# A two-layer GDN/mLSTM trunk on one core: the end written out in TensorE's order, the GDN heads' merge moved, and the second norm's factors two steps on

## The chip, the cores and the metric

The kernel runs on one core of a Trainium2 chip. The metric is the device time of one execution in microseconds (us). Its engines are TensorE (PE in the rows; its weight loads are PEld), VectorE (DVE), ScalarE (ACT), GpSimd (POOL) and SyncE (SP, which issues DMAs; SPq is the DMA queue it feeds). Each engine runs its own list of instructions in order and waits where an operand or a buffer is not ready.

## What is computed

Two residual layers over a sequence of 1024 tokens of width 1024, and a last RMSNorm. Layer 0 is a gated DeltaNet (GDN), layer 1 an mLSTM; each has 8 heads with keys of 128 and values of 256.

```python
for i in range(DEPTH):                       # 2
    h = rmsnorm(x, norm_w[i])
    x = x + (gdn_mixer if i % 2 == 0 else mlstm_mixer)(h, ...)
return rmsnorm(x, final_norm_w)
# gdn, chunked: per head and chunk
kk = einsum(k, k); a = I + tril(beta * kk * L, -1)
u, wk = triangular_solve(a, beta * v), triangular_solve(a, beta * exp(gc) * k)
attn = einsum(q, k) * L
w = u - wk @ S;  o = (q * exp(gc)) @ S + attn @ w;  S = decay * S + kd.T @ w     # scan
y = (rmsnorm(o) * silu(z)) @ w_out
```

## The kernel before

Tokens lie along the free axis in two halves of 512 (`half` 0 and 1), the width in eight blocks of 128 rows (`y0_0` to `y7_1` are the residual stream, block and half). A product in full precision is made of three matmuls on split operands (`hi`·`hi`, `lo`·`hi`, `hi`·`lo`) of 512 columns, over the blocks of the contraction.

The projections of all heads are one long row of such matmuls. Three of them are one **step**. After each step a planner, a table of step numbers per head (`KEYS`, `QUERIES`, `SOLVE`, `MERGE`, `TOKENS`, `SCAN`), lets generators issue a piece of the small work of that head: `gdn_keys` (transposes `tpk`, products `kk`, the decay matrix `nt`), `gdn_queries` (transposes `tpq`, their squares `sqrq` on ScalarE, products `kq`), `gdn_solve` (the inverse of the 32x32 diagonal blocks on VectorE, stored with the DMA `tb_dram` and read back as `td`), `gdn_merge` (per half: VectorE makes `tt` and `t` out of `td`, then four small products `xp`, `yp`, `xl`, `yl` put the blocks together, four steps apart), and `gdn_scan` of the head before (`ks`, `y`, `sn`, `o`, and `go`, which transposes the gated output). Each table has three entries: head 0, head 1 and heads 2 to 7. So the order of TensorE's instructions is the program's (`tc.manual_schedule` for PE), and the order on the other engines comes from a scheduler.

A PSUM bank tag names a pool of banks: `"d"` has two banks, `"c"` two and `"b"` one. `tpk`, `kk`, `tpq`, `kq`, `xp` to `yl`, `go` and the output products `out` all take turns on the two banks of `"d"`: a product waits until its bank's last reader is done.

`NORM1` holds the steps at which the second norm's column sums, factors and rows are issued, per half, in layer 0's output products; `prenorm` then needs its row product `n_rs`.

The end: the last head's output product of each block (`out_part`, `out`) and the other seven heads' (`out_heads`, `lout`, whose weights are split by ScalarE into `lw_hi` and by POOL into `lw_lo`) are added to the residual stream on VectorE. `finish(c0, c1)` is the last RMSNorm of columns c0 to c1 (of 8 blocks of 128 tokens): squares on ScalarE, their sum over the eight blocks on POOL (c0 of 0 and 4) or VectorE (6), a column sum on TensorE (`f_cs`), the factor (`f_rc`, with POOL's power), a diagonal matrix (`f_diag`), its row product (`f_rs`), and the multiplies with a DMA of each block. Here TensorE's order is the scheduler's; the program gives the order of the parts, in words whose letter o is `out_part`, h `out_heads` of half 1, a and b the two parts of `finish`:

```python
ORDER = "o0 a0 h1 b0 o4 a4 o6 a6 b4 b6"
```

The functions that the change touches, with the profile's line numbers:

Of the kernel before, what the change touches and what calls it, by code (L numbers as in the profile page):

```python
# [68 lines left out]
def hybrid_kernel(ctx, tc, x_in, norm_w, final_norm_w, gdn_w_in, gdn_conv_w, gdn_a_log, gdn_dt_bias, gdn_norm_w,  # L69
# [1330 lines left out]
    def finish(c0, c1):  # L1400

        ts, n = slice(c0 * P, c1 * P), c1 - c0
        accs = squares_of(c0, n, f"f{c0}", "k", QB, PF[c0])
# [6 lines left out]
        for k in range(KT):  # L1410
            if k in PM[c0]:
                G.tensor_tensor(x_of(k, c0, n), x_of(k, c0, n), rs_sb, ALU.mult)
            else:
                V.tensor_tensor(x_of(k, c0, n), x_of(k, c0, n), rs, ALU.mult)  # L1414
            nc.sync.dma_start(out[k * P:(k + 1) * P, ts], x_of(k, c0, n))
        yield
# [145 lines left out]
    sources.append(out_weights(mlstm_w_out, heads, (wp, "wraw", WB), "lw1"))  # L1562
    starts = [0] + [end for end, _ in LASTENDS]
    parts = {c0: finish(c0, c1) for c0, c1 in zip(starts, starts[1:])}
    for o in ORDER.split():
        if o[0] == "h":
            run(loads[1])
            run(out_heads(1, heads, gss[1], "lout"))
        elif o[0] == "o":
            c0 = int(o[1:])  # L1570
            out_part(st, c0, {0: 4, 4: 2, 6: 2}[c0])
        else:
            next(parts[int(o[1:])])
# [52 lines left out]
```

## Time and profile before

| what | value |
|---|---|
| time, median of 3 runs | 1971.52 us (1967.94 to 1972.74) |
| the profiled execution | 1967.29 us, span 1965.6 us |
| mean granted TensorE clock | 0.993 |
| busy: PE, DVE, ACT, POOL | 96%, 65%, 51%, 35% of the span |

The profile is of one execution, whose time is 0.65 us under the lowest of the three timed runs. Busy time is a sum of instruction durations; the span is from the first to the last instruction. The clock is TensorE's granted one as a share of 2.4 GHz. A row's idle time in brackets is that of its engine right before it.

### The profile page before, as it was taken

What the parts mean: (1) busy time and instruction counts of PE and PEld (TensorE: products, weight loads), DVE (VectorE), ACT (ScalarE), POOL (GpSimd) and SP (SyncE); (2) the same over time, 40 slices, a digit from 0 to 9 for tenths busy, and PEclk for the clock granted to TensorE, in tenths of its full rate; (3) what the DMA queues carried; (4) which work ended last, traced back from release to release, by engine and by line L of the source; (5) the groups of instructions that cost most, each with busy time, mean ns of one, the idle gap of its engine ahead of it and who ended that gap; (6) DMA issues with size and microseconds to landing.
All of it is one profiled execution on the core that took longest, in us unless ns stands there. A gap on an engine that the chain in (4) does not pass through costs nothing.

```text
span 1965.6 us, 28818 instructions
## 1 busy us (share of the span) xinstructions
PE 1886.7 (96%) x9768; PEld 1550.2 (79%) x9768; DVE 1271.1 (65%) x2877; ACT 1006.8 (51%) x2325; POOL 692.7 (35%) x621
## 2 busy tenths in 40 slices
PE   5998999999999999999999999999999999999987
PEld 3786787878787878787888788888888888878876
DVE  6678686858595959547555866666666666673313
ACT  5536454646465555545445554545554645564423
POOL 4234334333333334100121333333433333355553
PEclk9999999999999999999999999999999999999999
DMA  4211122121222222636421221212121221246332
GB/s 141 87 42 49 54 71 78 58 75 57 79 63 67 65 67 77 197 109 232 122 86 56 78 74 59 73 57 82 61 80 63 70 68 65 81 137 205 105 119 76
DMA packets 138620, 171.24 MB, mean 87 GB/s; under 512 B 30860, under 2 KB 68584, under 8 KB 138472
## 3 DMA queue, kind: packets, MB, share of 16 engines
q1 hardware_dynamic: 138472, 169.40, 27.5%
q8 instruction: 77, 1.26, 0.3%
q14 instruction: 71, 0.58, 0.1%
HBM read 142.87 MB, written 26.48 MB: 86 GB/s over the span
## 4 chain that ended last, share of the span: by engine, by line
PE 77%; DVE 10%; DMA 4%; ACT 3%; issue 2%; POOL 1%; SPq 1%; DVEq 0%; ACTq 0%; POOLq 0%
PE lout L679 8%; PE gkv_ps L480 7%; PE gout L679 7%; PE mkq_ps L480 7%; PE mv_ps L480 7%; PE mz_ps L480 6%; PE mog_ps L480 6%; PE gqv_ps L480 5%; PE gzp_ps L480 4%; PE mo L1455 1%; PE mv_ps L1212 1%; PE gv_ps L480 1%; PE o L1040 1%; PE y L1023 1%; PE out L384 1%
## 5 line engine op out<-in xcount | busy, mean ns | idle before, releaser
L394 POOL TENSOR_TENSOR g_r<-g_r,mhalf 128x1 f32<-128x1 f32 x64 | 41.4, 647 | 212.5 <-DVE g_r L393 192.4
L268 DVE SCALAR_TENSOR_TENSOR gw_lo<-gw_raw,rest,gw_hi 128x256 fp32r<-128x256 f32 x128 | 61.3, 516 | 66.0 <-ACT gw_hi L267 66.0
L263 POOL TENSOR_TENSOR lw_lo<-lw_raw,lw_hi 128x512 fp32r<-128x512 f32 x56 | 72.9, 1304 | 73.4 <-ACT lw_hi L262 69.9
L679 PE MATMUL lout<-lgp_hh,lw_hi 128*128 128x512 f32 x224 | 88.7, 396 | 4.6 <-DVE y L1414 3.2
L263 POOL TENSOR_TENSOR mog_lo<-mog_raw,mog_hi 128x512 fp32r<-128x512 f32 x39 | 50.3, 1290 | 115.3 <-ACT mog_hi L262 115.3
L263 POOL TENSOR_TENSOR mz_lo<-mz_raw,mz_hi 128x512 fp32r<-128x512 f32 x39 | 53.8, 1379 | 99.7 <-ACT mz_hi L262 99.7
L267 ACT ACTIVATE gw_hi<-gw_raw,rest 128x256 fp32r<-128x256 f32 x128 | 58.0, 501 | 58.3 <-PE gout L679 42.3
L679 PE MATMUL lout<-lgp_hl,lw_hi 128*128 128x512 f32 x224 | 87.7, 392 | 0.0
L679 PE MATMUL lout<-lgp_hh,lw_lo 128*128 128x512 f32 x224 | 86.8, 392 | 0.0
L263 POOL TENSOR_TENSOR mv_lo<-mv_raw,mv_hi 128x512 fp32r<-128x512 f32 x38 | 51.4, 1353 | 84.1 <-ACT mv_hi L262 53.1
L263 POOL TENSOR_TENSOR gkv_lo<-gkv_raw,gkv_hi 128x512 fp32r<-128x512 f32 x40 | 52.8, 1322 | 78.3 <-ACT gkv_hi L262 67.8
L480 PE MATMUL gkv_ps<-hh,gkv_hi 128*128 128x512 f32 x176 | 78.9, 448 | 0.0
L263 POOL TENSOR_TENSOR gzp_lo<-gzp_raw,gzp_hi 128x512 fp32r<-128x512 f32 x38 | 49.7, 1307 | 66.8 <-ACT gzp_hi L262 55.4
L262 ACT CAST lw_hi<-lw_raw 128x512 fp32r<-128x512 f32 x56 | 34.7, 620 | 73.7 <-PE lout L679 48.9
L263 POOL TENSOR_TENSOR mkq_lo<-mkq_raw,mkq_hi 128x512 fp32r<-128x512 f32 x35 | 45.6, 1302 | 75.9 <-ACT mkq_hi L262 64.8
L480 PE MATMUL gkv_ps<-hh,gkv_lo 128*128 128x512 f32 x176 | 69.2, 393 | 0.0
L480 PE MATMUL gkv_ps<-hl,gkv_hi 128*128 128x512 f32 x176 | 69.0, 392 | 0.0
L679 PE MATMUL gout<-glp_hh,gw_hi 128*128 128x512 f32 x160 | 66.7, 417 | 0.0
L394 POOL TENSOR_TENSOR m_r<-m_r,mhalf 128x1 f32<-128x1 f32 x64 | 42.6, 665 | 66.2 <-DVE m_r L393 65.2
L679 PE MATMUL gout<-glp_hl,gw_hi 128*128 128x512 f32 x160 | 62.7, 392 | 0.0
L679 PE MATMUL gout<-glp_hh,gw_lo 128*128 128x512 f32 x160 | 62.7, 392 | 0.0
L1043 ACT ACTIVATE gv_h<-o,g_r 128x256 f32<-128x256 f32 x64 | 30.3, 473 | 62.5 <-POOL g_r L394 61.8
(769 smaller groups left out, 6688.0 us busy)
## 6 DMA issues: line engine op xcount, KB each, us to landing
gw_raw<-in_gdn_w_out_dram SPq DMA_DIRECT2D x64, 256.0 KB, 2.7
lw_raw<-in_mlstm_w_out_dram SPq DMA_DIRECT2D x56, 256.0 KB, 2.7
gzp_raw<-in_gdn_w_in_dram SPq DMA_DIRECT2D x32, 256.0 KB, 3.2
...
```

What stands on the lines that cost most here:

```text
L262: A.copy(hi, raw)
L263: (e or G).tensor_tensor(lo, raw, hi.bitcast(F32), ALU.subtract)
L267: A.activation(hi[:, k], raw[:, k], AF.Copy, scale=c)
L268: V.scalar_tensor_tensor(lo[:, k], raw[:, k], c, hi.bitcast(F32)[:, k], ALU.mult, ALU.subtract)
L384: mm(ps, a[:, e, ds], b[:, e, hs], start=m == 0, stop=m == 3 * ET - 1)
L394: G.tensor_tensor(r, r, mhalf[:, :1], ALU.pow)
L480: mm(ps, w_[:, k, :], h_, start=first and k == 0 and i == 0, stop=k == 3 and i == 2, skip_group_check=True)
L679: mm(pss[2 * j + i], a[:, e, i * P:(i + 1) * P], b, start=h == heads[0] and e == 0 and m == 0, stop=h == heads[-1] and e == ET - 1 and m == 2)
L1023: mm(yp[:, :DV], st["tt"][half][:, cc, :], rr, start=True, stop=True)
L1040: mm(op[:, :DV], st["at"][half][:, cc, :], w, start=S is None, stop=True)
L1043: A.activation(v, op[:, :DV], AF.Copy, scale=r)
L1212: mm(ps[c], h_[k][half][:, c * P:(c + 1) * P], w_[:, k % 2, :], start=k == 0 and i == 0, stop=k == KT - 1 and i == 2)
```

## The change

Three things are changed.

1. **The end.** TensorE's order is now the program's there too: `out_part` 0 in one piece, then half 1's `lout` with the column sums and the row product of `finish(0, 4)` put between its groups of three matmuls (after 21 and after 51 of them), its multiplies and stores one by one after that; `out_part` 4; `out_part` 6 with the two products of `finish(4, 6)` inside; then `finish(6, 8)`. The sums and rows take banks of tag `"c"` in place of `"b"`. For `finish(6, 8)` the squares of blocks 6 and 7 are not added on VectorE: TensorE sums three parts per column (into `"c"` and `"d"`), and the factor is made per column. Its stores of odd blocks go out on ScalarE's DMA queue.
2. **The GDN tables.** The step numbers of `KEYS`, `QUERIES`, `SOLVE`, `MERGE`, `TOKENS` and `BLOCKS`.
3. **`NORM1`.** The first half's rows are asked for at step 8 in place of 6.

```diff
-NORM1 = ((-1, 4, 6), (-1, 9, 15))
+NORM1 = ((-1, 4, 8), (-1, 9, 15))
-ORDER = "o0 a0 h1 b0 o4 a4 o6 a6 b4 b6"
+F0STEPS = 6, 16
-KEYS = ((4, 9, 11, 14), (28, 31, 32, 35), (22, 25, 26, 29))
-QUERIES = ((17, 20, 22, 30), (68, 71, 76, 76), (82, 82, 86, 91))
-SOLVE = (27, 44, 32)
-MERGE = ((78, 82), (86, 93), (86, 100))
-TOKENS = ((37, 37, 81, 85), (71, 74, 97, 103), (64, 68, 107, 110))
+KEYS = ((2, 7, 8, 15), (32, 35, 36, 39), (22, 25, 26, 29))
+QUERIES = ((17, 20, 23, 30), (68, 71, 76, 76), (80, 80, 84, 89))
+SOLVE = (24, 44, 32)
+MERGE = ((78, 82), (86, 89), (88, 100))
+TOKENS = ((37, 37, 81, 85), (71, 74, 97, 103), (64, 74, 107, 110))
-BLOCKS = (101, 115, 114, 132)
+BLOCKS = (101, 115, 114, 126)
...
+            if k in own:
+                accs[k] = sq
+            elif e in accs:
-                e.tensor_tensor(accs[e], accs[e], sq, ALU.add)
...
+    def column_sums(accs, name, tags):
+        css = [pwork(f"{name}_cs{c}", tag)[:, :1] for c, tag in enumerate(tags)]
+        for i, acc in enumerate(accs):
+            for c, cs in enumerate(css):
+                mm(cs, acc[:, c * P:(c + 1) * P], ones[:, :1], start=i == 0, stop=i == len(accs) - 1)
+        return css
...
-    def finish(c0, c1):
+    def finish(c0, c1, after=None):
+        own = (6, 7) if c1 == NT else ()
...
+        yield
+        sums = column_sums(accs, f"f{c0}", "cd") if own else sums_of(accs, f"f{c0}", "c")
+        diag = rstd_of(sums, f"f{c0}", bool(own))
+        yield
+        rs = rows_of(diag, f"f{c0}", "c")
...
+        with tc.issue_after(after()) if after else nullcontext():
+            for k in range(KT):
...
+                (nc.scalar if own and k % 2 else nc.sync).dma_start(out[k * P:(k + 1) * P, ts], x_of(k, c0, n))
+                if c1 <= HT:
+                    yield
...
+    with tc.manual_schedule(engines={mybir.EngineType.PE}):
+        sources.append(out_weights(mlstm_w_out, heads, (wp, "wraw", WB), "lw1"))
+        run(loads[1])
+        f0, f4, f6 = finish(0, 4), finish(4, 6, lambda: added[0].ins), finish(6, 8)
+        run(out_part(st, 0, 4))
+        do(f0)
+        for n, _ in enumerate(out_heads(1, heads, gss[1], "lout")):
+            if n == F0STEPS[0]:
+                do(f0)
+            if n >= F0STEPS[1] and n % 2 == 0:
+                do(f0)
+        run(out_part(st, 4, 2))
+        do(f4)
+        for n, _ in enumerate(out_part(st, 6, 2)):
+            if n in (1, 5):
+                do(f4)
+        do(f6); do(f6); run(f4); run(f6)
```

In the rows below a tile's name carries head and half or chunk (`xp4_0`: head 4, half 0; `ks3_7`: head 3, chunk 7).

**First place, merge of heads 2 to 7, here head 4.** TensorE before, from the transpose `go3_5` of head 3's scan on (left out are eight and three 512-column matmuls of head 4's projection):

```order
L356 MATMUL go3_5_gp_5296<-ident_117,gv3_h1_4526 128x128 x2
L480 MATMUL gzp4_ps7_5204<-hh0_4_1_425,gzp4_4_hi_5205 128x512
...
L480 MATMUL gzp4_ps7_5204<-hh0_6_1_435,gzp4_4_lo_5206 128x512
L971 MATMUL xp4_0_5314<-t4_0_5250,nt4_0_4624 32x32 x8
L849 MATMUL tpq4_1_5326<-ident_117,gqT4_1_5063 128x128 x4
...
L1018 MATMUL ks3_7_5344<-S3_6_5285,gkT3_1_3444 128x256
```

And now:

```order
L372 MATMUL go3_5_gp_5291<-ident_117,gv3_h1_4526 128x128 x2
L500 MATMUL gzp4_ps7_5204<-hh0_4_1_425,gzp4_4_hi_5205 128x512
...
L869 MATMUL tpq4_1_5308<-ident_117,gqT4_1_5063 128x128 x4
...
L500 MATMUL gzp4_ps7_5204<-hh0_7_1_440,gzp4_4_lo_5206 128x512
L1038 MATMUL ks3_7_5332<-S3_6_5280,gkT3_1_3444 128x256
L500 MATMUL gkv5_ps00_5336<-hh0_0_0_233,gkv5_00_hi_5232 128x512
L500 MATMUL gkv5_ps00_5336<-hl0_0_0_234,gkv5_00_hi_5232 128x512
L500 MATMUL gkv5_ps00_5336<-hh0_0_0_233,gkv5_00_lo_5233 128x512
L991 MATMUL xp4_0_5346<-t4_0_5304,nt4_0_4624 32x32 x8
L500 MATMUL gkv5_ps00_5336<-hh0_1_0_238,gkv5_00_hi_5232 128x512
...
L940 MATMUL kq4_1_5361<-gqT4_1_5063,gkT4_1_4472 128x128 x4
```

`tpq4_1` and `ks3_7` now stand ahead of `xp4_0`, which six more 512-column matmuls precede as well, and `kq4_1` comes three matmuls behind it. On ScalarE at the same place, before (the last products' reads `xs`, the squares `sqrq`, the scan's output `gv3_h1`):

```order
L392 ACTIVATE g3_6_sq_5291,g3_6_r_5290<-o3_6_5287 128x256
L1043 ACTIVATE gv3_h1_4526<-o3_6_5287,g3_6_r_5290 128x256
L977 COPY xs4_0_5323<-xp4_0_5314 32x128
L852 ACTIVATE sqrq4_1_5331,sq4_5254<-tpq4_1_5326 128x128 x2
L262 CAST gkv5_02_hi_5351<-gkv5_raw1_5000 128x512
L852 ACTIVATE sqrq4_1_5331,sq4_5254<-tpq4_1_5326 128x128 x2
```

And now:

```order
L412 ACTIVATE g3_6_sq_5286,g3_6_r_5285<-o3_6_5282 128x256
L872 ACTIVATE sqrq4_1_5313,sq4_5243<-tpq4_1_5308 128x128 x2
L1063 ACTIVATE gv3_h1_4526<-o3_6_5282,g3_6_r_5285 128x256
L872 ACTIVATE sqrq4_1_5313,sq4_5243<-tpq4_1_5308 128x128 x2
L278 CAST gkv5_02_hi_5339<-gkv5_raw1_5000 128x512
L997 COPY xs4_0_5355<-xp4_0_5346 32x128
```

Two of the four squares of `tpq4_1` now run ahead of the scan's scaled copy `gv3_h1`, two behind it, and `xs4_0` comes last.

**Second place, head 1's keys.** VectorE before, up to head 1's first `nt` (`kd1` multiplies `tpk1_0` out of its bank, `hs` are sums of the shared operands, `b1` and `nb1` small factors):

```order
L886 TENSOR_SCALAR nb1_1427<-b1_1425 128x4
L458 TENSOR_TENSOR hs1_1_1760<-hs1_1_1760,x1_0_77 128x512
L299 SCALAR_TENSOR_TENSOR gvT1_0_1_1476<-gkv1_ps11_1279,gcw_159,gvT1_0_1_1476 128x509
L301 TENSOR_TENSOR gvT1_0_1_1476<-gvT1_0_1_1476,gv1_0_edge_285 128x3
L894 SCALAR_TENSOR_TENSOR nt1_0_1493<-kk1_0_1488,nb1_1427,at1_0_1443 128x128 x4
L873 TENSOR_TENSOR kd1_1429<-tpk1_1_1520,ekd_277 128x512
L883 TENSOR_SCALAR sk1_1424<-sk1_1424 128x4
```

And now:

```order
L898 TENSOR_TENSOR at1_1_1549<-growb01_1_1547,cmask_128 128x512
L458 TENSOR_TENSOR S2hl1_1773<-hs1_1_1760,S2hh1_1772 128x512
L893 TENSOR_TENSOR kd1_1476<-tpk1_0_1477,ekd_277 128x512
L903 TENSOR_SCALAR sk1_1471<-sk1_1471 128x4
L477 TENSOR_TENSOR hs2_0_1789<-x2_1_80,x2_0_79 128x512
L904 RECIPROCAL b1_1472<-sk1_1471 128x4
L478 TENSOR_TENSOR hs2_1_1790<-hs2_1_1790,x2_0_79 128x512
L905 TENSOR_TENSOR b1_1472<-b1_1472,beta_273 128x4
L906 TENSOR_SCALAR nb1_1474<-b1_1472 128x4
L914 SCALAR_TENSOR_TENSOR nt1_0_1519<-kk1_0_1514,nb1_1474,at1_0_1490 128x128 x4
```

`kd1` of `tpk1_0` stood sixteen rows ahead of `nt1_0` and now stands seven rows ahead of it, behind three of the shared sums.

**Third place, the end.** TensorE before around the two products of `finish(0, 4)` (`f0_cs`, `f0_rs`):

```order
L384 MATMUL out4_1_19304<-mg7_1_lo_18021,wo0_hi_18141 128x256
L384 MATMUL out4_1_19304<-mg7_1_hi_18020,wo0_lo_18142 128x256
L223 MATMUL f0_cs_18662<-ones_122,f0_sq0_18631 128x1 x4
L242 MATMUL f0_rs_18672<-f0_diag_18670,ones_122 128x512
L679 MATMUL lout1_02_18760<-lgp1_00_hh_18676,lw1_1_0_hi_18770 128x512
L679 MATMUL lout1_02_18760<-lgp1_00_hl_18677,lw1_1_0_hi_18770 128x512
```

And now:

```order
L699 MATMUL lout1_03_18751<-lgp1_00_hh_18571,lw1_1_0_lo_18761 128x512
L235 MATMUL f0_cs_18797<-ones_122,f0_sq0_18717 128x1 x4
L699 MATMUL lout1_03_18751<-lgp1_01_hh_18577,lw1_1_0_hi_18760 128x512
...
L699 MATMUL lout1_00_18748<-lgp1_20_hh_18595,lw1_0_2_lo_18813 128x512
L258 MATMUL f0_rs_18855<-f0_diag_18805,ones_122 128x512
L699 MATMUL lout1_00_18748<-lgp1_21_hh_18601,lw1_0_2_hi_18812 128x512
```

They stood in one place with nothing between them, ahead of half 1's `lout` (apart from what the scheduler had put further ahead); now `lout` matmuls stand ahead of, between and behind them. VectorE before, from the multiplies of columns 4 and 5 to the factor `f6_rc`:

```order
L1414 TENSOR_TENSOR y1_1_18425<-y1_1_18425,f4_rs_19399 128x256
...
L1414 TENSOR_TENSOR y6_1_18435<-y6_1_18435,f4_rs_19399 128x256
L386 TENSOR_TENSOR y7_1_18437<-y7_1_18437,out6_7_19457 128x256
L1414 TENSOR_TENSOR y7_1_18437<-y7_1_18437,f4_rs_19399 128x256
L212 TENSOR_TENSOR f6_sq0_19465<-f6_sq0_19465,f6_sq6_19482 128x256
L212 TENSOR_TENSOR f6_sq0_19465<-f6_sq0_19465,f6_sq7_19485 128x256
L230 TENSOR_SCALAR f6_rc_19499<-f6_cs_19496 128x2
```

And now:

```order
L404 TENSOR_TENSOR y7_1_18437<-y7_1_18437,out6_7_19459 128x256
L1440 TENSOR_TENSOR y1_1_18425<-y1_1_18425,f4_rs_19449 128x256
...
L1440 TENSOR_TENSOR y7_1_18437<-y7_1_18437,f4_rs_19449 128x256
L244 TENSOR_SCALAR f6_rc_19504<-f6_cs0_19496 128x1
L244 TENSOR_SCALAR f6_rc_19504<-f6_cs1_19497 128x1
L251 TENSOR_TENSOR f6_diag_19508<-ident_117,f6_rc_19504 128x256
```

The two additions of squares are gone, `y7_1`'s addition of `out6_7` stands ahead of the multiplies, and the factor is made in two instructions.

## Rows read from the trace of the kernel before

**Rows 1.** Part 1 of the page: each engine's busy time, its share of the span, and its instructions.

```profile
PE 1886.7 (96%) x9768; PEld 1550.2 (79%) x9768; DVE 1271.1 (65%) x2877; ACT 1006.8 (51%) x2325; POOL 692.7 (35%) x621
```

**Rows 2.** The waits of TensorE over the whole span. Columns: the instruction that waited, what it waited for, us in total, times, the longest in us.

```profile
PE xp L971 <- DVE t L962: 12.7, 6, 2.6
...
PE n_rs L242 <- DVE n_diag L235: 4.5, 2, 3.4
PE kk L891 <- DVE nt L894: 4.1, 1, 4.1
...
PE f_rs L242 <- DVE f_diag L235: 3.7, 2, 2.2
PE lout L679 <- DVE y L1414: 3.2, 1, 3.2
PE f_cs L223 <- DVE f_sq L212: 2.7, 1, 2.7
...
PE y L1023 <- DVE xr L942: 2.1, 1, 2.1
...
PE kk L891 <- DVE kd L873: 0.7, 1, 0.7
```

**Rows 3.** The windows view for TensorE: stretches named by their start and end in us. Columns: length, busy us of TensorE (instructions), granted clock (1.00 is 2.4 GHz, 0.50 is 1.2 GHz), DMA share, GB/s.

```profile
161.60:165.00 3.40, 3.40 (x12) 0.50 0.14 19
320.20:323.60 3.40, 3.39 (x31) 1.00 0.02 5
414.20:417.60 3.40, 3.10 (x24) 0.50 0.13 39
793.10:796.40 3.30, 3.30 (x11) 0.50 0.36 120
1871.70:1878.50 6.80, 3.61 (x8) 0.50 0.59 220
```

**Rows 4.** The timeline from 405 to 421 us, in head 3's projections, with head 3's queries and the first merge products at its right, and head 2's scan between them. Columns: start us, us, engine, line, operation, tiles, shapes, count, and in brackets the engine's idle time before it and what ended it.

```profile
406.14 0.60 PE L849 MATMUL tpq<-ident,gqT 128*128 128x128 f32 x4
...
406.57 1.06 PE L920 MATMUL kq<-gqT,gkT 128*128 128x128 f32 x8
...
411.29 0.39 PE L480 MATMUL gzp_ps<-hl,gzp_hi 128*128 128x512 f32 x1
...
411.51 0.39 PE L480 MATMUL gzp_ps<-hh,gzp_lo 128*128 128x512 f32 x1
412.46 0.69 DVE L959 TENSOR_TENSOR tt<-td,dmask 128x512 f32<-128x512 f32 x1 [2.46 <-DMA td<-tb_dram]
...
413.92 0.43 DVE L962 STREAM_TRANSPOSE t<-tt 64x256 f32<-64x256 f32 x1
...
414.08 1.25 POOL L394 TENSOR_TENSOR g_r<-g_r,mhalf 128x1 f32<-128x1 f32 x1 [3.76 <-DVE g_r L393]
...
414.50 0.64 PE L971 MATMUL xp<-t,nt 32*32 32x32 f32 x16 [2.60 <-DVE t L962]
...
415.36 0.47 ACT L1043 ACTIVATE gv_h<-o,g_r 128x256 f32<-128x256 f32 x1 [4.75 <-POOL g_r L394]
...
416.28 0.28 ACT L852 ACTIVATE sqrq<-tpq 128x128 bf16<-128x128 f32 x1 [0.16 <-PE tpq L849]
```

**Rows 5.** The same view at the same place one head earlier (head 2), two rows.

```profile
312.86 0.54 POOL L394 TENSOR_TENSOR g_r<-g_r,mhalf 128x1 f32<-128x1 f32 x1 [0.72 <-DVE g_r L393]
...
320.21 0.44 PE L971 MATMUL xp<-t,nt 32*32 32x32 f32 x16 [2.10 <-DVE t L962]
```

**Rows 6.** The timeline at 72 to 75 us, where the tables of cumulated decays (`gcs`, `gr_sb`, `dec`) are made, just ahead of head 0's keys.

```profile
72.45 0.28 DVE L785 COPY gr_sb<-gr_ps 64x128 f32<-64x128 f32 x1 [0.39 <-PE gr_ps L783]
...
74.18 0.23 ACT L781 ACTIVATE dec<-cum 128x64 f32<-128x64 f32 x1
```

**Rows 7.** The windows view of all engines from 149 to 187 us, head 1's keys. Columns: length, then busy us (instructions) of TensorE, its weight loads, VectorE, ScalarE and POOL, the granted clock, DMA share, GB/s.

```profile
149.00:187.00 38.00, 30.65 (x142) 24.27 (x141) 32.86 (x75) 23.74 (x60) 18.51 (x14) 0.96 0.21 59
```

**Rows 8.** The timeline inside that window, where head 1's `nt`, `kd` and second `kk` lie.

```profile
160.39 1.11 DVE L894 SCALAR_TENSOR_TENSOR nt<-kk,nb,at 128x128 f32<-128x128 f32 x4
...
161.43 0.67 DVE L873 TENSOR_TENSOR kd<-tpk,ekd 128x512 f32<-128x512 f32 x1
...
161.56 2.07 PE L891 MATMUL kk<-gkT 128*128 128x128 f32 x8 [4.11 <-DVE nt L894]
```

**Rows 9.** The timeline of POOL in the end, two rows: an add of the final norm's squares, and the four multiplies of half 0's output.

```profile
1866.42 1.29 POOL L212 TENSOR_TENSOR f_sq<-f_sq,f_sq 128x512 f32<-128x512 f32 x1 [1.05 <-ACT f_sq L210]
...
1873.07 4.96 POOL L1412 TENSOR_TENSOR y<-y,f_rs_sb 128x512 f32<-128x512 f32 x4 [2.95 <-ACT f_rs_sb L1409]
```

**Rows 10.** The timeline from 1952 us, the final norm of the last two column blocks.

```profile
1952.13 1.41 DVE L1414 TENSOR_TENSOR y<-y,f_rs 128x256 f32<-128x256 f32 x4
...
1955.15 0.61 PE L223 MATMUL f_cs<-ones,f_sq 128*128 128x1 f32 x4 [2.74 <-DVE f_sq L212]
1955.79 0.16 DVE L230 TENSOR_SCALAR f_rc<-f_cs 128x2 f32<-128x2 f32 x1 [0.70 <-PE f_cs L223]
...
1957.33 1.19 PE L242 MATMUL f_rs<-f_diag,ones 128*128 128x256 f32 x2 [1.58 <-DVE f_diag L235]
...
1958.96 2.40 DVE L1414 TENSOR_TENSOR y<-y,f_rs 128x256 f32<-128x256 f32 x7 [1.78 <-ACT f_rs_sb L1409]
```

**Rows 11.** The timeline of the DMA queue that SyncE issues, from 1959 us: the last eight output stores.

```profile
1959.41 3.77 SPq L1415 DMA_DIRECT2D out_dram<-y  x8
```

More of the change, by code (lines that the diff above doesn't have):

```diff
@@ L201, in h_tile, with squares_of @@
         return big.tile([P, TH], F32R, tag=h_tag(part, k, half), name=name)
-    def squares_of(c0, n, name, tag, bufs, pool=()):
+    def squares_of(c0, n, name, tag, bufs, pool=(), own=()):
         accs = {}
@@ L224, in sums_of, with rstd_of @@
         return [cs[:, i * n:(i + 1) * n] for i in range(len(accs))]
-    def rstd_of(sums, name):
-        n = sums[0].shape[1]
+    def rstd_of(sums, name, columns=False):
+        n = len(sums) if columns else sums[0].shape[1]
         rc = sp.tile([P, HT], F32, tag="rc", name=f"{name}_rc")[:, :n]
-        V.tensor_scalar(rc, sums[0], 1.0 / D, EPS, ALU.mult, ALU.add)
-        for cs in sums[1:]:
-            V.scalar_tensor_tensor(rc, cs, 1.0 / D, rc, ALU.mult, ALU.add)
+        if columns:
+            for c, cs in enumerate(sums):
+                V.tensor_scalar(rc[:, c:c + 1], cs, 1.0 / D, EPS, ALU.mult, ALU.add)
+        else:
+            V.tensor_scalar(rc, sums[0], 1.0 / D, EPS, ALU.mult, ALU.add)
+            for cs in sums[1:]:
+                V.scalar_tensor_tensor(rc, cs, 1.0 / D, rc, ALU.mult, ALU.add)
         G.tensor_tensor(rc, rc, mhalf[:, :n], ALU.pow)
@@ L385, in out_part @@
                     m += 1
-            V.tensor_tensor(x_of(d, c0, n), x_of(d, c0, n), ps, ALU.add)
+            added[0] = V.tensor_tensor(x_of(d, c0, n), x_of(d, c0, n), ps, ALU.add)
+    added = {}
     def rms_factor(o_ps, extra, name):
@@ L1398, in mlstm_prepare @@
             yield
-    def finish(c0, c1):
+    def finish(c0, c1, after=None):
         ts, n = slice(c0 * P, c1 * P), c1 - c0
-        accs = squares_of(c0, n, f"f{c0}", "k", QB, PF[c0])
+        own = (6, 7) if c1 == NT else ()
+        accs = squares_of(c0, n, f"f{c0}", "k", QB, PF[c0], own)
         for k in range(KT):
             A.activation(x_of(k, c0, n), x_of(k, c0, n), AF.Copy, scale=fwc[:, k:k + 1])
-        rs = rows_of(rstd_of(sums_of(accs, f"f{c0}"), f"f{c0}"), f"f{c0}")
+        yield
[3 more added lines that the diff above has]
+        rs = rows_of(diag, f"f{c0}", "c")
         yield
@@ L1409, in finish @@
         A.copy(rs_sb, rs)
[L1410 to L1416, printed above, removed]
+        with tc.issue_after(after()) if after else nullcontext():
+            for k in range(KT):
+                if k in PM[c0]:
+                    G.tensor_tensor(x_of(k, c0, n), x_of(k, c0, n), rs_sb, ALU.mult)
+                else:
+                    V.tensor_tensor(x_of(k, c0, n), x_of(k, c0, n), rs, ALU.mult)
+                (nc.scalar if own and k % 2 else nc.sync).dma_start(out[k * P:(k + 1) * P, ts], x_of(k, c0, n))
+                if c1 <= HT:
+                    yield
     def mlstm_scan(h, st):
@@ L1561, in hybrid_kernel @@
                     do(scan)
[L1562 to L1573, printed above, removed]
+    with tc.manual_schedule(engines={mybir.EngineType.PE}):
[14 more added lines that the diff above has]
+                do(f4)
+        do(f6)
+        do(f6)
+        run(f4)
+        run(f6)
 _INS = ['x', 'norm_w', 'final_norm_w', 'gdn_w_in', 'gdn_conv_w', 'gdn_a_log', 'gdn_dt_bias', 'gdn_norm_w', 'gdn_w_out',
```

2 lines of the change are left out of this document (1 added, 1 removed).

## Prediction

> **What bounds the kernel now.** Read the busy table first: TensorE works 1886.7 of 1965.6 us [rows 1], VectorE 65%, so the span falls only where TensorE waits (78.9 us in all, start-up and the tail with it) or runs at the lower clock. Then its table of waits [rows 2]: the largest item that comes again and again is `xp`, the first merge product of heads 2 to 7, 12.7 us in six waits on VectorE's transpose `t`; next a `kk` of head 1 (4.1), and the end's `f_rs`, `lout` and `f_cs` (3.7, 3.2, 2.7). Last the windows view for the clock [rows 3]: after several of these waits TensorE ran about 3.4 us at 1.2 GHz.
>
> **Merge of heads 2 to 7.** Head 3's timeline [rows 4] shows the chain: the inverse comes back by DMA at 412.46, VectorE makes `tt`, two other results and `t` (412.46 to 414.35), and `xp` starts at 414.50 after 2.60 of idleness, so TensorE was there at 411.90. The order now puts six 512-column matmuls, `tpq` and `ks` ahead of `xp` (first place). A 512-column matmul costs 0.22 (411.29 to 411.51), `tpq` 0.43 (406.14 to 406.57), `ks` is taken like `tpq`: 6 x 0.22 + 0.43 + 0.43 = 2.2 us. TensorE now comes at 414.1, `t` is there at 414.5 at the latest: 0.4 left here, nothing where the wait was under 2.2. The six waits add up to 12.7; the longest is 2.6, so at most about 0.4 each stays in two or three heads. VectorE's order around `t` is unchanged, so `t` doesn't recede with TensorE.
>
> What is late next: `kq` of half 1, three matmuls behind `xp`. It takes the bank of `tpq` of half 1, which ScalarE must have squared four times; two squares now stand behind `gv_h`, which waits for POOL's power `g_r`. In head 3 the power ends at 415.33 and `gv_h` at 415.83 [rows 4]; two squares of 0.28 with their accumulator reads follow, about 0.8 by estimate: 416.6. TensorE gets to `kq` at 414.3 + 0.43 + 0.66 = 415.4. That is a wait of up to 1.2 in head 3, where POOL took 1.25; in head 2 it took 0.54 [rows 5], and the other heads stand nearer to that. I put 2.2 us of new waits over all six heads, between 0 and 1 us for each (6). What else the two steps move, `yp`, `xl` and `yl`, goes with `xp`; the spare time behind them is not in the rows, which is the bound above.
>
> The clock: of the six waits, 2.60 (head 3) was followed by 3.4 us at 0.50, with 3.10 busy, and another such stretch stands at 793.1 with 3.30 [rows 3]; work at half rate loses half of its time, 1.55 + 1.65 = 3.2 us. The wait of 2.10 in head 2 [rows 5] was followed by full clock [rows 3]. With waits around 1 us I expect neither stretch. Sum: 12.7 + 3.2 - 2.2 = 13.7 us saved, 10 to 16.
>
> The Trainium skill, in "TensorE: Matmul & The Clock Gate", section "Part 1: The HAM clock gate (the "warmup" mystery)", says that the gate's watching runs free and doesn't start with a pause. No row here tells that apart; by the page the 3.2 us could come back at another pause, with 10.5 us in place of 13.7 by it.
>
> **Head 0.** `tpk` now stands right behind `gr_ps` and takes its bank, free after VectorE's copy: 0.39 idle and 0.28 copy [rows 6]. TensorE loses about 0.4 (the rest is `gr_ps` itself). If it waits for the decay tables instead, 74.41 less 72.4, it is 2.0. I take 0.4.
>
> **Head 1.** Waits of 0.7 and 4.1 and half a clock stretch, 3.4 x 0.5 = 1.7, lie here now [rows 2, 3]: 6.5 us. From 149 to 187 us VectorE works 32.86 of 38.00 us [rows 7], so no order of the same work can save more than its idle 5.1. The second `kk` waits for `nt` (1.11), behind a full queue, with `kd` next to it [rows 8]. The new order (second place) puts `kd` of half 0 behind three more shared sums; until it ends, `tpk` of half 1 can't have its bank, and then `nt` of half 0 and `kd` of half 1 hold up the second `kk`. Counting the rows ahead, `kd` comes some 3 us later than TensorE wants the bank and the second `kk` about 1 us: 4 us of waits in place of 4.8, and perhaps no low clock. I take 2.5 us saved, between 0 and 5.1.
>
> **Second norm.** `n_rs` waits 4.5 - 3.4 = 1.1 us for `n_diag` the second time [rows 2]. Two steps are six matmuls, 1.3 us at least: the wait goes, 1.1 saved, and nothing behind it is waited for before layer 1.
>
> **The end, half 0.** `f_rs` waits 2.2 and the next `lout` 3.2 (its bank is freed by the multiplies) [rows 2], and 3.61 us of busy time lie in 6.8 us at 0.50 [rows 3], worth 1.8. The sums and rows now lie behind 21 and 51 `lout` matmuls (third place), 4.6 and 11 us behind `out_part`, and `lout` no longer needs the norm's bank: 2.2 + 3.2 + 1.8 = 7.2 saved. Price: POOL. It adds seven squares at 1.29 [rows 9], 9.0 us, and these can follow `out_part` at its own pace, but its splits `lw_lo` take turns with them; and its four multiplies (4.96) stand ahead of a split. I take 0.5 us of new waits, between 0 and 4.
>
> **The tail.** TensorE's last product ended at 1952.41 (2.74 before `f_cs`), and VectorE's `f_rc` began at 1955.79, 3.38 later [rows 10]: five multiplies and two additions of squares stood between. Now only the addition of `out6_7` and five multiplies do. At 1.41 for four [rows 10], five take 1.75; with the addition, about 0.4 like them, 2.2. From there on the chain is as it was: 1.1 saved (0.5 to 2.0). The stores: one queue issues eight in 3.77 from 1959.41 on [rows 11], to 1963.18, while the last multiply ends at 1961.36 [rows 10]; on two queues the last issue can follow it by one store, 0.47: 1961.8, about 1.3 less. No row shows ScalarE issuing; I take 1.0, between 0 and 1.3.
>
> By these rows it is issuing that ends last: the last store is issued 1.8 us after the last multiply. The Trainium skill, in "DMA: Bandwidth & Descriptors", section "Issuing engines are not separate DMA queues", speaks against a second queue, since all transfers share the same engines and only the time of issuing is saved. By that rule, too, the saving is at most the 1.3 worked out above.
>
> End and tail: 7.2 - 0.5 + 1.1 + 1.0 = 8.8.
>
> **Sum.** 13.7 - 0.4 + 2.5 + 1.1 + 8.8 = 25.7 us. The profiled execution took 1967.3, 4.2 under the median; on its base the change gives 1941.6, on the median's 1945.8. I say 1945.5. A difference of 0.3% (5.9 us) is about what a measurement here can tell from none.
>
> **Rivals.**
> - *The merge's wait only changes places.* Each of the six heads waits 2 us at `kq` or later (the scan's `y` and `go`, ScalarE's queue) and the clock stays as it is: 13.7 becomes 12.7 - 12 = 0.7, time 1958.5. For it: head 3's 1.2. Against it: POOL's 0.54 in head 2. Chance 0.12.
> - *POOL starves the end.* Its splits come 4 us late while squares and multiplies go first, and the clock falls once more (1.7): end 8.8 becomes 3.6, time 1951. For it: 9.0 us of adds beside the splits; against it: POOL is at 35% [rows 1]. Chance 0.12.
> - *Head 1 is VectorE's and gains nothing, and the clock drops elsewhere*, at two of the pauses that stay: 25.7 - 2.5 - 3.2 = 20, time 1951. For it: a low stretch follows 4.11 in head 1, 2.60 in head 3 and none 2.10 in head 2 [rows 3, 5, 8], so pauses of 2 to 4 us, as head 1 may keep, can go either way. Chance 0.12. The Trainium skill's page on the clock, named above, has this case: its free-running watch.
> - *The change does little*: VectorE's `t` follows TensorE because the transposes ahead of it wait for `go`, which is moved too; the end alone is left: 1971.5 - 10 = 1961.5. Against it: VectorE's order there is the same and its chain starts with the DMA [rows 4]. Chance 0.04.
> - *Slower.* ScalarE's squares and the scan block each other: `gv_h` waits for POOL, the squares behind it hold the bank, TensorE stops at `kq`, and the scan's next `ks` and `y` behind it come late too. Everything else gains 12.7 + 3.2 + 12 = 27.9; it takes 4.7 us in each of six heads to eat that and 5.6 to be 0.3% slower. Head 3's worst row gives 1.2. At 6 us each: 1979.5. Chance 0.03.
>
> My forecast (saved 21 to 31 us, 1940.5 to 1950.5 by the terms' ends) has 0.57. The range reaches over the first rival's middle and the two at 1951: 1937 to 1957, down from 1940.5 by the 4.2 between profile and median. Faster 0.91: all but the slow case, half of the fourth, and a part of the first that gets worse; same 0.05; slower 0.04.
>
> **What would show it.** Right: `xp` gone from the top of the waits, `kq` with a total near 2; granted clock 1.00 at head 3 and head 7; `n_rs` with one wait; `f_rs` once, in the tail; the last TensorE product of `out` to the span's end 11 us in place of 13.2. Wrong: waits of `kq`, `ks` or `y` on ScalarE of 2 us in most heads; `lout` waiting for POOL's `lw_lo`; a `tpk` in head 1 waiting over 4 us for `kd` with a low clock behind it.

## The result and the profile after

The change takes 1947.11 us, median of 4 runs (1945.22 to 1947.92), where the kernel before takes 1971.76 in the same series: the ratio is 0.9877, 95% interval 0.986 to 0.9894. That is 24.7 us less; 1945.5 was predicted, and 25.7 less. The sum came out, but two of its terms did not, with errors of opposite sign, so that it came out this close is luck. The profiled execution of after took 1947.53 us with a span of 1945.8 and a mean granted clock of 0.991, against 1965.6 and 0.993 before (the table ahead of the change): the two profiles lie 19.8 us apart.

Part 1 of the page after, to be read beside [rows 1]:

```profile
PE 1889.4 (97%) x9776; PEld 1552.1 (80%) x9776; DVE 1269.6 (65%) x2876; ACT 1009.4 (52%) x2325; POOL 687.7 (35%) x621
```

TensorE is busy as long as before (1889.4); what went is idleness. Its waits after, with the columns of [rows 2]:

```profile
PE tpk L869 <- DVE kd L893: 4.5, 2, 3.5
...
PE n_rs L258 <- DVE n_diag L251: 3.4, 1, 3.4
...
PE f_rs L258 <- DVE f_diag L251: 1.8, 1, 1.8
...
PE yp L991 <- DVE tt L1004: 1.6, 1, 1.6
...
PE f_cs L235 <- POOL f_sq L216: 1.0, 1, 1.0
...
PE tpk L869 <- DVE gr_sb L805: 0.4, 1, 0.4
...
PE f_cs L226 <- DVE f_sq L216: 0.2, 1, 0.2
```

`xp` on `t`, 12.7 us before, is gone. `n_rs` waits once, in the first norm (3.4), no longer a second time. `f_rs` waits once, in the tail, `lout` no longer for the norm. The two waits of `kk` in head 1 (4.1 and 0.7 in [rows 2]) are gone too. New are `tpk` behind `kd` in head 1 (3.5 of the 4.5; the other 1.0, in head 2, was there before), a `yp` in head 1 and small ones.

Where between first and last instruction the time went is read from four products that both orders have: the first and the last `kk` that waits for a merge's `tt`, the first `mg` of the mLSTM layer, and a late `mo` just ahead of the end. First before, then after, from TensorE's timelines:

```profile
351.41 0.82 PE L891 MATMUL kk<-gkT 128*128 128x128 f32 x5 [0.37 <-DVE tt L992]
...
729.42 0.82 PE L891 MATMUL kk<-gkT 128*128 128x128 f32 x5 [0.53 <-DVE tt L992]
...
1090.83 0.94 PE L1389 MATMUL mg<-mqT,mkT 128*128 128x128 f32 x6 [2.44 <-DVE mkd_lo L1380]
...
1764.12 0.70 PE L1455 MATMUL mo<-mS,mqT 128*128 128x258 f32 x2 [0.92 <-ACT mo_g L1463]
```

```profile
354.32 0.94 PE L911 MATMUL kk<-gkT 128*128 128x128 f32 x6 [0.48 <-DVE tt L1012]
...
722.05 1.16 PE L911 MATMUL kk<-gkT 128*128 128x128 f32 x8 [0.35 <-DVE tt L1012]
...
1077.66 0.65 PE L1409 MATMUL mg<-mqT,mkT 128*128 128x128 f32 x3 [2.42 <-DVE mkd_lo L1400]
...
1753.05 0.70 PE L1482 MATMUL mo<-mS,mqT 128*128 128x258 f32 x2 [0.56 <-ACT mo_g L1490]
```

Up to the first of them the change loses 2.9 us (351.41 to 354.32), although the wait of 2.1 in head 2 [rows 5] is gone: heads 0 and 1, with the start of the kernel ahead of them, lose 5.0. From there to the last `kk`, four merges later, it gains 378.01 - 367.73 = 10.3. From there to `mg`, with head 7's merge and the second norm, 361.41 - 355.61 = 5.8. In the mLSTM layer, which isn't touched, it loses 675.39 - 673.29 = 2.1. From `mo` to the end of the span it gains 201.48 - 192.75 = 8.7.

| term | predicted | these two profiles |
|---|---|---|
| merge, heads 2 to 7 | -13.7 | -16.6 (2.1 + 10.3 + 4.2 of the 5.8) |
| heads 0 and 1, with the start | -2.1 | +5.0 |
| second norm | -1.1 | -1.1, with 0.5 more in that stretch |
| mLSTM layer | 0 | +2.1 |
| end and tail | -8.8 | -8.7 |

(Head 7's 4.2 is its wait of 2.52, the last of the six, and half of the low-clock stretch at 793 [rows 3].)

### The profile page after: what moved, and what is told of

Read it like the earlier page. It is cut to its first block, busy times and chain, and to the rows that moved or that the text cites. A ratio compares the mean times of both kernels' runs of the same rounds, so it can differ in the third digit from the quotient of the medians.

```text
span 1945.8 us, 28819 instructions
## 1 busy us (share of the span) xinstructions
PE 1889.4 (97%) x9776; PEld 1552.1 (80%) x9776; DVE 1269.6 (65%) x2876; ACT 1009.4 (52%) x2325; POOL 687.7 (35%) x621
## 4 chain that ended last, share of the span: by engine, by line
PE 85%; DVE 6%; ACT 3%; DMA 3%; issue 1%; POOL 1%; SPq 0%; DVEq 0%; ACTq 0%; POOLq 0%
PE gout L699 9%; PE lout L699 8%; PE gzp_ps L500 7%; PE gkv_ps L500 7%; PE mkq_ps L500 7%; PE mv_ps L500 7%; PE mz_ps L500 6%; PE gqv_ps L500 6%; PE mog_ps L500 6%; PE mo L1482 1%; PE o L1060 1%; PE mv_ps L1232 1%; PE y L1043 1%; PE gv_ps L500 1%; PE sn L1050 1%; PE ks L1038 1%
## 5 line engine op out<-in xcount | busy, mean ns | idle before, releaser
L279 POOL TENSOR_TENSOR gqv_lo<-gqv_raw,gqv_hi 128x512 fp32r<-128x512 f32 x30 | 38.6, 1287 | 65.3 <-PE sn L1050 25.2
```

The source lines that it names most:

```text
L279: (e or G).tensor_tensor(lo, raw, hi.bitcast(F32), ALU.subtract)
```

## The experiments

All are single-core runs; the ratio is to the kernel before on the same chip at the same time, which took 1977.0 us (median of 7 runs) beside the first four, 1978.0 beside the next four and 1975.5 beside the ninth to eleventh. Kernels that ran beside different runs of before are better compared by their ratios.

| run | what it is | median us | ratio | 95% interval |
|---|---|---|---|---|
| e1_end_only | tables and `NORM1` old | 1965.57 | 0.9938 | 0.9921 to 0.9956 |
| e2_tables_only | end old | 1955.26 | 0.9892 | 0.9877 to 0.9907 |
| e3_heads01_old | heads 0 and 1 old | 1943.72 | 0.9832 | 0.9817 to 0.9847 |
| e4_merge_only | heads 2 to 7 alone new | 1957.78 | 0.9896 | 0.9875 to 0.9916 |
| e5_changed_again | the change | 1946.67 | 0.9842 | 0.9821 to 0.9864 |
| e6_merge1_old | head 1's second merge old | 1942.90 | 0.9830 | 0.9811 to 0.9848 |
| e7_keys1_old | head 1's keys old | 1946.46 | 0.9849 | 0.9827 to 0.9871 |
| e8_head0_old | head 0 old | 1943.86 | 0.9836 | 0.9817 to 0.9854 |
| e9_merge1_head0_old | e6 and e8 together | 1942.20 | 0.9814 | 0.9783 to 0.9845 |
| e10_one_queue, e11_sums_on_vector, e12_before_again | one execution each | 1948.45, 1947.72, 1975.72 | - | - |

### The parts apart: e1, e2, e4

The edits, as constants. e1 is the changed file with `NORM1` and all six lines of step numbers as before (two of the seven are shown):

```diff
-NORM1 = ((-1, 4, 8), (-1, 9, 15))
+NORM1 = ((-1, 4, 6), (-1, 9, 15))
-KEYS = ((2, 7, 8, 15), (32, 35, 36, 39), ...
+KEYS = ((4, 9, 11, 14), (28, 31, 32, 35), ...
...
```

> Only the end is new; the GDN tables and the second norm's step are those of before. Theory A (where the two traces put the time: the end 8.8 us, heads 2 to 7 about 16, the second norm 1.4, heads 0 and 1 a loss of about 5) and theory B (the prediction's terms: end 8.8, heads 2 to 7 13.7, norm 1.1, heads 0 and 1 a gain of 2.1) both expect 8.8 us less than before, about 1963 us. Rival: the end's gain hangs on the earlier arrival from the GDN layer and is gone without it: 1968 us or more.

Measured 1965.57, 11.5 us less than before. The end's gain stands on its own; the rival is out. It is more than the 8.8 that both theories had, by less than the interval (0.9921 to 0.9956 is 8.7 to 15.6 us). The traces show the end by itself: from the late `mo` of the section on the result to the end of the span it is 192.3 us in e1's profile, 201.5 in the first profile of before and in e2's, and 203.4 in e4's and e12's, which also have the old end and whose low stretch there is 10.2 us long where [rows 3] has 6.8. So the new end is worth 9.2 to 11.1 us, by how long that stretch is.

e2 is the file before with the new tables and `NORM1`.

> Only the GDN tables and the second norm's step are new; the end is that of before. Theory A: -16 - 1.4 + 5 = 12.4 us less than before, about 1959 us. Theory B: -13.7 - 1.1 - 2.1 = 16.9 us less, about 1955 us.

Measured 1955.26: theory B's number, but against a kernel before that had become 5.3 us slower, so that the gain, 21.8 us, is more than either had. The absolute times of the two theories had assumed 1971.8 for before. With e1's 11.5 it makes 33.3; the whole change gives 31.3 beside its own runs of before (e5), so within the intervals the two parts add.

e4 is the file before with three entries:

```diff
-QUERIES = (..., (82, 82, 86, 91))
-MERGE = (..., (86, 100))
-TOKENS = (..., (64, 68, 107, 110))
+QUERIES = (..., (80, 80, 84, 89))
+MERGE = (..., (88, 100))
+TOKENS = (..., (64, 74, 107, 110))
```

> The kernel before with only the entries of heads 2 to 7 in QUERIES, MERGE and TOKENS new. Theory A: 16 us less than before, about 1956 us, with no wait of kq over 0.5 us. Theory B: 13.7 us less, about 1958 us, with about 2 us of new waits at kq of half 1. Rival (the wait only changes places): within 3 us of before, 1969 us or more.

Measured 1957.78, 19.3 us less than before by the medians, 20.6 by the ratio. The rival (the wait only changes places) is refuted. In its waits `xp` on `t` and `kq` do not occur; the largest that is left at heads 2 to 7 is one that was there before:

```profile
PE kk L891 <- DVE tt L992: 3.4, 5, 0.7
```

From the first to the last of the `kk` above it takes 368.6 us in e4's profile and 367.7 to 368.9 in the ten others with these entries, against 378.0, 380.2 and 382.0 in the three without them (before, e1, e12). So three table entries for heads 2 to 7 carry most of the change, and their worth depends on what before is on the day: about 16 us in the first two profiles, 20 here. No run takes the three entries apart.

### Why before differs: e12

> The kernel before, once more, for a second profile: beside the experiments it took 1973 to 1984 us with a mean granted clock of 0.985 to 0.989, in the first profile 1967 us at 0.993. Theory A (the same waits, more of them followed by a low-clock stretch): the same six waits of xp, 12.7 us in all within 1 us, and low stretches of 3.4 us behind four to six of them in place of two, and behind the waits of head 1 and the mLSTM layer. Theory B (other waits): sum of the waits of xp off by over 3 us, or low stretches where TensorE had not waited.

It took 1975.72 us, clock 0.987, span 1974.0. The waits of `xp` in it:

```profile
PE xp L971 <- DVE t L962: 13.2, 6, 2.7
```

The same waits as in [rows 2], within 0.5 us. The clock behind five of them (windows view, columns of [rows 3]; the stretch at 417 reads like its neighbours):

```profile
321.50:324.80 3.30, 3.30 (x11) 0.50 0.02 5
...
513.00:516.40 3.40, 3.34 (x31) 1.00 0.14 41
608.20:611.50 3.30, 3.30 (x9) 0.50 0.00 0
703.80:707.10 3.30, 3.30 (x9) 0.50 0.03 7
799.30:802.60 3.30, 3.30 (x23) 0.50 0.47 146
```

Five of six are followed by 3.3 us or more at 1.2 GHz, in the first profile two of six. The sixth, head 4's at 513, had waited 2.37 and kept its clock; head 6's had waited less and lost it:

```profile
702.46 0.44 PE L971 MATMUL xp<-t,nt 32*32 32x32 f32 x16 [1.75 <-DVE t L962]
```

Theory A holds: the waits are the same, the clock behind them isn't. Each such stretch with 3.3 us of work costs half of it, 1.65 us, so the three more are 5 us of the 8.4 between the two profiles of before. Two more low stretches, at 51.8 us and behind the wait of `mg` at 1096.3, and the longer one in the end are 5 us by the same working, more than the rest. The 22 timed runs of before beside the experiments have clocks of 0.983 to 0.989, where the first profile had 0.993. They took 1972.2 to 1984.1 us, the four beside the result 1967.9 to 1972.7: the two groups hardly overlap, and why the later ones lose their clock more often, by chance or by something that they have in common, is not shown.

### Heads 0 and 1: e3, e5 to e9

Head 1 in the changed kernel first: its `yp` waits for VectorE,

```profile
231.20 0.18 PE L991 MATMUL yp<-xs,tt 32*32 32x32 f32 x1 [1.57 <-DVE tt L1004]
```

and the clock around it and in heads 0 and 1, before (the one stretch that [rows 3] lacks) and after:

```profile
72.90:76.20 3.30, 3.30 (x11) 0.50 0.08 20
```

```profile
50.70:54.10 3.40, 3.40 (x10) 0.50 0.00 0
71.20:77.90 6.70, 6.02 (x16) 0.50 0.16 56
160.00:166.70 6.70, 5.90 (x16) 0.50 0.15 44
231.60:238.30 6.70, 6.70 (x25) 0.50 0.14 39
414.00:417.40 3.40, 3.40 (x31) 1.00 0.18 54
1078.10:1081.40 3.30, 3.30 (x13) 0.50 0.76 251
```

Before, two low stretches with 3.30 and 3.40 us of work [rows 3 for the second]; after, three of twice the length, with 6.02, 5.90 and 6.70. Half of the difference is 6.0 us. A fourth, of 3.40, lies at 50.7, ahead of head 0's keys, where the profile before had full clock: 1.7 more. So the clock costs 7.7 and all else gains 2.7; that is the loss of 5.0, and 1.7 of it comes from ahead of the two heads. Behind the place of head 3's merge (414) the clock is full now. The stretch at 1078 follows the same wait of `mg` as before (2.42 and 2.44, in the two fences of products above), which had no low clock then: this is most of the loss in the untouched mLSTM layer (e11, whose program is the same up to the end, has no low clock there and takes 673.5 from `mg` to `mo`, as before).

> The changed kernel with the entries of heads 0 and 1 in the five tables, and BLOCKS, as before. Theory A: heads 0 and 1 lost 5 us by the change, so 5 us less than the changed kernel, about 1942 us. Theory B: they gained 2.1, so 2.1 us more, about 1949 us. In the trace, theory A expects the low-clock stretches at 72 us and 162 us to be 3.4 us long again, as before, and none near 230 us.

e3's edit is e1's, for the first two entries of each table and `BLOCKS` alone. Measured 1943.72, 0.9832 of before; the change beside its own runs of before (e5) is 0.9842, so by time no difference is clear of the intervals. Its profile has

```profile
163.20:166.50 3.30, 3.30 (x13) 0.50 0.14 20
230.00:238.00 8.00, 7.64 (x80) 1.00 0.13 33
```

one stretch of 3.3 us at head 1, full clock at 230, as theory A had expected; two more of 3.4 lie near 50 and near 88 us rather than at 72.

> The changed kernel as it is, on the chip of the next three, for their comparison and for a second profile. Both theories: 0.9877 of before, about 1947 us. Theory A (the low-clock stretch that followed the merge of head 1 near 231 us comes with its wait there) expects the 1.6 us wait of yp and a low stretch behind it again; theory B (low stretches fall where they fall) expects them in other places than in the first profile.

Measured 0.9842 of before in place of 0.9877: the change is the same (1946.7 and 1947.1 us), before is slower here. The second profile has the wait of `yp` (1.57) and a low stretch of 6.8 us behind it again, and its other low stretches lie where those of the first profile do. But one of its four runs took 1940.65 us at a clock of 0.997. By estimate (the missing share of the clock, doubled, times the span) that is about 12 us at 1.2 GHz in all, where the profiled execution, at 0.991, has 35: most of these stretches are missing in that run.

> The changed kernel with head 1's second merge at step 93 again in place of 89. Theory A (the loss in heads 0 and 1 is this merge: the 1.6 us wait of yp on VectorE and the 6.8 us at low clock behind it): 4 to 5 us less than the changed kernel, as much as putting all entries of heads 0 and 1 back gave. Rival (the loss is head 1's keys, whose tpk waits 3.5 us for kd): within 1 us of the changed kernel.

```diff
-MERGE = ((78, 82), (86, 89), (88, 100))
+MERGE = ((78, 82), (86, 93), (88, 100))
```

Measured 1942.90, 3.8 us under e5, a little less than theory A expected, and with ratios of 0.9830 and 0.9842 not clear of the intervals. In its profile `yp` doesn't wait for `tt`; an `xp` of head 1 does, for ScalarE, and the clock stays full:

```profile
228.85 0.44 PE L991 MATMUL xp<-t,nt 32*32 32x32 f32 x16 [1.39 <-ACT gz L843]
```

```profile
229.00:236.00 7.00, 6.64 (x76) 1.00 0.13 37
```

In the same profile the stretches near 72 and 160 us are 3.4 long in place of 6.8, and the one near 50 is missing; these lie ahead of the merge, which can't have moved them. So a part of the 3.8 need not be the merge's.

> The changed kernel with head 1's keys at steps 28, 31, 32, 35 again. Theory A (the merge is the loss): within 1 us of the changed kernel. Rival (head 1's keys are): 3 us less than the changed kernel. The prediction's step had 2.5 us gained here, so 2.5 us more.

```diff
-KEYS = ((2, 7, 8, 15), (32, 35, 36, 39), (22, 25, 26, 29))
+KEYS = ((2, 7, 8, 15), (28, 31, 32, 35), (22, 25, 26, 29))
```

Measured 1946.46, 0.2 us from e5: neither the 2.5 us predicted nor a loss shows. The interval, 0.9827 to 0.9871, is 8.7 us wide, so 2.5 us either way isn't ruled out.

> The changed kernel with head 0's entries in KEYS, QUERIES and SOLVE as before. Both traces put tpk of head 0 right behind gr_ps now, with 0.4 us of waiting and a low-clock stretch of 6.8 us in place of 3.4: theory A (this belongs to the new steps) expects 1 to 2 us less than the changed kernel; theory B (the stretch's length is chance) expects no difference over 1 us, with the wait of tpq for kd near 87 us, 2.1 us, back.

The edit is e3's, for head 0's entries of `KEYS`, `QUERIES` and `SOLVE`. Measured 1943.86, 2.8 us under e5, more than either theory had. The wait of `tpq` for `kd` near 87 us is back, 2.2. Its profile has no low stretch at 161 or 231 either, places whose steps the edit doesn't touch (but `yp` waits 0.93 there in place of 1.57), so this difference is no proof against head 0's steps.

> The changed kernel with head 1's second merge at step 93 and head 0's entries in KEYS, QUERIES and SOLVE as before; only head 1's keys stay new. Theory A (both new places cost time by themselves, 3.8 and 2.8 us in the runs with one of them put back): 6.6 us less than the changed kernel, 0.981 of before. Theory B (what they cost is the low-clock stretches that happen to follow their waits, and one stretch less in a run is all that each gave): no better than either alone, 0.983 to 0.984 of before.

Measured 1942.20, 0.9814: between the two theories (0.981 and 0.983 to 0.984), and its interval holds both. It is not shown that the two places add.

The traces separate these versions better than the times. When the first of the `kk` above starts, in each profile:

| heads 0 and 1 | profiles | start of that `kk`, us |
|---|---|---|
| new | result, e2, e5, e10, e11 | 354.3, 355.0, 354.2, 354.3, 352.5 |
| new, but head 1's keys old | e7 | 352.6 |
| new, but head 0 old | e8 | 353.5 |
| head 1's second merge old | e6, e9 | 350.0, 351.0 |
| all old (heads 2 to 7 new) | e3, e4 | 351.0, 351.2 |

Every profile with the new merge is later than every one without it, by 1.3 us or more; putting back the keys or head 0 alone doesn't do it. In the five with all entries new `yp` waits 1.57 or 1.58 us each time, with a low stretch behind it each time, of 6.8 us in three and 3.4 in two. With e7's and e8's entries it waits 1.07 and 0.93, and with the old merge not at all for `tt`, and there is no low clock at that place. So the traces, one of each version, put the loss at head 1's second merge, four steps too early. By the table its size is 1.3 to 5.0 us, and part of that is which low stretches an execution has. No version here is faster than the change clear of the intervals; e9, e6 and e3 have the lowest medians, 3 to 4.5 us under it, and all are clear of the kernel before.

### The tail: e10, e11

> The changed kernel with all stores of the end on SyncE's queue. Read in the trace, not in the time: from the last product of out to the end of the span 11.0 us in the changed kernel. Theory A (issuing ends last, the prediction's 1.0 us): about 12 us. Theory B (the transfers or their landing end last, whoever issues them): 11.0 us.

```diff
-(nc.scalar if own and k % 2 else nc.sync).dma_start(out...)
+nc.sync.dma_start(out...)
```

The stores issued by SyncE in this run, ten of them from 1938.03 on:

```profile
1938.03 6.32 SPq L1441 DMA_DIRECT2D out_dram<-y  x10
```

The last is issued at 1944.35 and the span ends at 1946.7. From the last product of `out` to the end it is 11.8 us, against 11.0. From `f_rs` (1938.47 here, 1938.31 in the changed kernel) to the end it is 8.23 us, against 7.49: the second queue is worth 0.74. Theory A's sign, three quarters of its size. After the last issue there are 2.35 us to the end here; with two queues the last issue ends at 1942.74 and the end comes 3.1 us later. So a part of what issuing gives is taken back before the end.

> The changed kernel with the squares of blocks 6 and 7 of the last columns added on VectorE again (the column sums, their banks and the two queues stay). Read in the trace: from the last product of out to VectorE's factor f_rc 2.0 us in the changed kernel. Theory A (VectorE's queue, five multiplies and what else stands there, ends last): two more additions of 0.42, so about 2.8 us. Theory B (the wait is ScalarE's last square): 2.0 to 2.3 us.

The edit is `own = ()`, with the column sums and the two queues as they are. Three instructions of the tail:

```profile
1933.29 1.74 DVE L1440 TENSOR_TENSOR y<-y,f_rs 128x256 f32<-128x256 f32 x5
...
1934.95 0.95 DVE L216 TENSOR_TENSOR f_sq<-f_sq,f_sq 128x256 f32<-128x256 f32 x2
...
1936.04 0.98 PE L226 MATMUL f_cs<-ones,f_sq 128*128 128x1 f32 x4 [3.12 <-DVE f_sq L216]
```

TensorE's last product of `out` ended at 1936.04 - 3.12 = 1932.92; the factor's first part starts at 1936.63, 3.7 us later, against 2.0 in the changed kernel. Both theories were low. The two additions don't stand ahead of the five multiplies but behind them (1934.95), so they come after both the multiplies and ScalarE's squares. From the last product to the end it is 13.1 us, against 11.0: the sums on TensorE are worth 2.0 in this order. The prediction's 1.1 was against the order before, in which the same five multiplies stood ahead of the additions, but the first of them began 0.28 us ahead of the end of the last product (1952.13 [rows 10] and 1952.41) and here begins 0.37 behind it. There `f_rc` came 3.38 behind the last product; the change made it 1.35 less in place of 1.1.

## Why the prediction was right, and where not

**The merge.** Right that the wait goes and the clock with it; the new wait at `kq`, 2.2 us in the sum, was wrong: there is none over 0.2 (its start for TensorE, 414.3, was also no time that the sum before it gives; with `xp` at 414.5 the wait in head 3 would have been 1.0, not 1.2). These 2.2 are most of the 2.9 by which this term was too small. The step that failed took head 3's VectorE and ScalarE at their old times while TensorE's moved. The timeline before (SyncE's queue and the scan's `y`, a fixed point in both orders) and after:

```profile
403.20 0.81 SPq L490 DMA_DIRECT2D gqv_raw<-in_gdn_w_in_dram  x2
...
404.10 0.38 SPq L947 DMA_DIRECT2D tb_dram<-xr  x1
...
404.33 0.59 PE L1023 MATMUL y<-rr,tt 128*128 128x256 f32 x2
...
407.36 2.77 SPq L950 DMA_DIRECT2D td<-tb_dram  x4
```

```profile
406.21 0.33 SPq L967 DMA_DIRECT2D tb_dram<-xr  x1
...
406.63 0.88 SPq L510 DMA_DIRECT2D gqv_raw<-in_gdn_w_in_dram  x2
...
407.15 0.59 PE L1043 MATMUL y<-rr,tt 128*128 128x256 f32 x2
...
407.97 3.38 SPq L970 DMA_DIRECT2D td<-tb_dram  x4
...
412.29 0.38 PE L372 MATMUL go_gp<-ident,gv_h 128*128 128x128 f32 x2
...
412.98 0.69 DVE L979 TENSOR_TENSOR tt<-td,dmask 128x512 f32<-128x512 f32 x1 [0.70 <-DMA td<-tb_dram]
...
414.44 0.43 DVE L982 STREAM_TRANSPOSE t<-tt 64x256 f32<-64x256 f32 x1
...
414.60 1.25 POOL L414 TENSOR_TENSOR g_r<-g_r,mhalf 128x1 f32<-128x1 f32 x1 [1.61 <-DVE g_r L413]
...
416.65 0.28 ACT L872 ACTIVATE sqrq<-tpq 128x128 bf16<-128x128 f32 x1
...
416.97 0.44 PE L991 MATMUL xp<-t,nt 32*32 32x32 f32 x16
...
418.14 1.05 PE L940 MATMUL kq<-gqT,gkT 128*128 128x128 f32 x8
```

Before, the store `tb_dram` was issued behind two loads of `gqv_raw` of 256 KB each, and `td`, which has to wait for its landing, 3.26 us after it. Now it is issued ahead of them, and `td` follows 1.76 us after it. Against `y`, `td` is issued 0.8 us later in place of 3.0. So VectorE's `t` is ready at 414.87, 2.1 ahead of `xp` (416.97), where the prediction had it 0.4 late; `g_r` behind it in VectorE's and POOL's queues is earlier by as much, and the last square ends at 416.93, 1.2 ahead of `kq` at 418.14. `xp` came 4.7 us after `go`, as worked out (2.4 + 2.2). The gain is thus two moves, TensorE's arrival later and the DMA's earlier; of the second the prediction had nothing, although it is a change in the order of SyncE's queue. The other heads bear it out: in heads 2 to 6 `td` follows the store after 2.4 to 3.3 us before and after 1.75 to 2.4 now, and `t` is ready 1.5 to 2.2 ahead of `xp`. In head 7 no load of `gqv_raw` stands ahead of the store in either order, and `t` is ready at 784.88 for an `xp` at 785.02, just in time by TensorE's move alone. No run has one move without the other, so what each is worth in time is not shown.

**The clock.** 3.2 us were put in as a fixed term. e12 shows that it is not fixed: the same six waits had two low stretches in one execution and five in another. What the change removed is the occasion for all of them; the gain is 19.8 us between the first two profiles and 31 beside e5, by what before drew.

**Heads 0 and 1.** A gain of 2.1 was predicted. The waits are as the prediction counted them, 0.4 for head 0's `tpk`, 3.5 for head 1's (3 predicted), and 1.0 for the second `kk` is not there. What was wrong is "perhaps no low clock": three long stretches cost more than two short ones (the windows in the section on heads 0 and 1), and the new wait of `yp`, from moving the second merge four steps ahead, stood in no term. The traces put the loss at that merge (the table in the section on heads 0 and 1); the times, with intervals of 0.2%, show neither the loss nor its size.

**Second norm.** Right: one wait less, and the stretch around it gains 1.1 and 0.5 more.

**The end.** Right in sum (8.7 for 8.8). POOL's price showed as a wait of 1.0 at `f4`'s column sums, not at the splits. The waits of `f_rs` and `lout` and the low clock of that place are gone. In the tail, `f_rc` starts 2.0 us after the last product, which ended 0.24 ahead of `f_cs`, at 1934.77 (2.2 predicted), and it is 11.0 to the end (11.1 predicted):

```profile
1936.80 0.22 DVE L244 TENSOR_SCALAR f_rc<-f_cs 128x1 f32<-128x1 f32 x2
...
1938.31 1.22 PE L258 MATMUL f_rs<-f_diag,ones 128*128 128x256 f32 x2 [1.83 <-DVE f_diag L251]
...
1939.97 2.40 DVE L1440 TENSOR_TENSOR y<-y,f_rs 128x256 f32<-128x256 f32 x7 [1.72 <-ACT f_rs_sb L1434]
...
1940.42 2.32 ACTq L1441 DMA_DIRECT2D out_dram<-y  x4
```

**The rivals.** "The wait only changes places" and "the change does little" fell with e4, "POOL starves the end" with e1, "slower" with the result. (The range's lower end, 1940.5 less 4.2, is 1936.3 rather than the 1937 stated; nothing hangs on it.) "Head 1 gains nothing and the clock drops elsewhere" is, in its mechanism, what happened, on top of a merge that gave more. The Trainium skill's rule in "TensorE: Matmul & The Clock Gate", section "Part 1: The HAM clock gate (the "warmup" mystery)", that the gate's watching runs free, fits e12: the same waits, other stretches. The Trainium skill's other rule, in "DMA: Bandwidth & Descriptors", section "Issuing engines are not separate DMA queues", fits e10: 0.74 us, and no more than the 1.6 by which the last issue ends earlier (1942.74 for 1944.35).
